# Two layers of a hybrid streaming-encoder trunk: the recurrence paced one channel tile a slot, splits of the indexer queries queued a unit later, key copies moved to VectorE

## The chip, the core and the metric

The kernel runs on one core of one Trainium2 chip. The metric is the device time of one execution in microseconds (us), measured around the whole program; below it is given as the median of three executions. The engines are TensorE (PE; its weight loads are listed apart as PEld), VectorE (DVE), ScalarE (ACT), GpSimd (POOL) and SyncE (SP), which here issues nearly all DMAs.

## What is computed

Two layers over a sequence of 512 tokens with 1024 channels, in fp32. Each layer normalises the input, projects it once into ten pieces and runs three branches: (A) a gMLP gate, (B) sparse attention, in which a small relu indexer picks 128 keys for each query, (C) a gated linear recurrence (RG-LRU). The branches are projected, gated, summed and projected back; a ConvFFN follows. Cut to the lines that matter for the change:

```python
gu, gv, q, k, v, qi, ki, wi, lx, lg = jnp.split(h @ w_in[l], IN_SPLITS, axis=-1)
# (B) the indexer: 8 heads of 64, one shared key
qi = apply_rope(qi.reshape(bsz, seq, IDX_HEADS, IDX_DIM), cos_i, sin_i)
ki = apply_rope(ki[:, :, None, :], cos_i, sin_i)[:, :, 0, :]
logits = jnp.einsum('bqhd,bsd->bqhs', qib, ki) * (IDX_DIM ** -0.5)
score = jnp.einsum('bqhs,bqh->bqs', jax.nn.relu(logits), wib) * (IDX_HEADS ** -0.5)
...
# (C) the recurrence, on xc = causal_dwconv(lx, conv_w, conv_b)
r = jax.nn.sigmoid(einsum(xg, w_r) + b_r)
i = jax.nn.sigmoid(einsum(xg, w_i) + b_i)
log_a = -LRU_C * r * softplus(-lam)
a = jnp.exp(log_a)
b = jnp.sqrt(-jnp.expm1(2.0 * log_a)) * (i * xc)
h_t = a_t * h_(t-1) + b_t          # associative_scan over the sequence
y_c = h * jax.nn.gelu(lg)
```

## The kernel before, in words

**Products and weights.** Activations lie with channels on the 128 partitions and the 512 tokens along the free axis, as four or eight channel tiles. An fp32 operand is split into two fp32r halves, high and low, and `mm3` (L127 to L132) makes each product of three fp32r matmuls: high by high (L130), high by low (L131), low by high (L132; which operand is the weight differs by the phase). `mm` (L124 to L126) is a plain fp32 matmul; the recurrence's gates use it. All weights come as a stream of units, one 512 KB tile each: `Stream` (L144) loads a tile through SP's DMA queue into one of six staging buffers `wst`, copies it on ACT to `wh` (the high half) and subtracts on DVE to get `wl` (the low half), five units ahead of its use, in six buffers. A unit is 24 matmuls of 512 columns. Within a layer the units come in this order: lx (4), qi (4), ki, v (4), lg (4), gv (4), gu (4), the gates and projections of branch C, k and q (8), the branches A and B, wo, up, dn. Results land in PSUM, a pool of eight banks that are handed out in turn; a matmul into a bank waits until what was read from it before has been read. Helpers record most elementwise work, so the profile names the helper's line: L104 is ACT's `act`, L109 its `copy`, L112 `tt` (`tensor_tensor`, on DVE unless POOL is passed as `G_`; a `split` is a copy and a `tt`), L116 `ts`, L121 `stt`.

**Order of the work.** After nearly every unit the program calls `B.pump(budget)` (L214). Each call is a slot: generators that were added as background tasks run in their order until the budget is spent. A task that yields a positive number has used that much of the budget; one that yields -n sleeps n slots. A low task, the modulation rows of a later norm (`mod_task`, L309), advances one accumulation (L121, 128x1024) a slot. The order of the instructions on each engine is the order in which this program writes them.

**The stretch that the change touches** (`layer`, L767). The lx units make the four tiles `xc` through a causal convolution. Then the recurrence `lru` (L595) is added as a background task and sleeps four slots. Each of the four qi units runs `rope` (L524): two 64-row copies on ACT from PSUM, a product on DVE, a product and a sum on POOL. The sum is then split: a copy on ACT, a subtraction on POOL. The ki unit (L795 to L810) does a rope for the single key, copies the indexer weights `wr`, splits the key, and makes from each half two masked keys: `k0` by a scale on ACT, `k1` by a memset on POOL and two 32-row copies on ACT. Four v units follow; their four banks collect all tokens over all four units. After each of the first three the slot has a budget of 5.0. The lg units make the gate of the recurrence.

**The recurrence** computes for each tile two gate matmuls (L601) into two banks with a sigmoid each (ACT, L603), then exponentials and tangents hyperbolic (L610, L611), a maximum and a root (L615, L616), two products and the scan (L619 to L622), and, when lg is there, the product with it and a split. With its sleep of four and budgets of 2.0 and 5.0, tiles 0 and 1 get their gates behind ki, tiles 2 and 3 behind v0. The `indexer` (L534) sleeps three slots from ki on, transposes `wr` (L540 copies it from PSUM), and then makes the scores of three query blocks i = 1, 2, 3 with 128 (i + 1) columns: for each head a product of three matmuls, a ReLU on ACT and an accumulation on DVE; a copy of the score row on ACT (L561) ends a block. The choice of the 128 largest follows on DVE.

Of the kernel before, what the change touches and what calls it, by code (L numbers as in the profile page):

```python
# [67 lines left out]
def trunk_kernel(ctx: ExitStack, tc: tile.TileContext, x, cc, wm, wu, cp, rows, gmw, gmb, lruw, cst, out):  # L68
# [17 lines left out]
    V, A_, G_, T_ = nc.vector, nc.scalar, nc.gpsimd, nc.tensor  # L86
# [6 lines left out]
    def S(dt=F32, shape=None):  # L93
        return sp.tile(shape or [P, 512], dt, tag="S", name=nm("s"), bufs=NS)
# [13 lines left out]
    def copy(o, i, scale=1.0):  # L108
        A_.activation(o, i, AF.Copy, scale=scale)  # L109

    def tt(o, a, b, op, eng=None):
        (eng or V).tensor_tensor(o, a, b, op)  # L112
# [7 lines left out]
    def stt(o, a, s, b, op0, op1):  # L120
        V.scalar_tensor_tensor(o, a, s, b, op0=op0, op1=op1)  # L121

    M, AD, SU = ALU.mult, ALU.add, ALU.subtract
# [130 lines left out]
    cos_i, sin_i = ks[:, K_CI:K_CI + 512], ks[:, K_SI:K_SI + 512]  # L254
# [141 lines left out]
    def col(kind, budget=2.0):  # L396
        if carry:
            p = carry.pop(0)
            return p
        p = bank()  # L400
        w = W.get(kind)
        cm(p, w)
        return p
# [120 lines left out]
    def rope(p, cs, sn):  # L524
        r = S()
        copy(r[0:64], p[64:128])
        copy(r[64:128], p[0:64])
        d = S()
        tt(d, p, cs, M)
        tt(r, r, sn, M, G_)  # L530
        tt(d, d, r, AD, G_)
        return d
# [61 lines left out]

    def lru(xc, lw, s84, wts, gl, res):  # L595
        rr, ii = [], []
        yield -4
        for t in range(4):
            for wi_, ob, lst in ((0, O_BR, rr), (1, O_BI, ii)):
                p = bank()  # L600
                mm(p, wts[wi_][:, t * P:(t + 1) * P], xc[t], True, True)  # L601
                o = S()
                act(o, p, AF.Sigmoid, bias=lw[:, ob + t:ob + t + 1])  # L603
                lst.append(o)
            yield 1.2
        aa = []
        for t in range(4):
            tt(ii[t], ii[t], xc[t], M, G_)
            a = S()
            act(a, rr[t], AF.Exp, scale=s84[:, t:t + 1])  # L610
            act(rr[t], rr[t], AF.Tanh, scale=s84[:, 4 + t:5 + t])  # L611
            aa.append(a)
            yield 1.2
        for t in range(4):
            V.tensor_scalar(rr[t], rr[t], 1e-34, None, op0=ALU.max)  # L615
            act(rr[t], rr[t], AF.Sqrt)  # L616
            yield 0.6
        for t in range(4):
            stt(rr[t], aa[t], 1.0, rr[t], AD, M)  # L619
            tt(ii[t], ii[t], rr[t], M)  # L620
            yield 1.2
            V.tensor_tensor_scan(xc[t], aa[t], ii[t], 0.0, M, AD)  # L622
            yield 0.6
        while len(gl) < 4:
            yield -1
        for t in range(4):
            tt(xc[t], xc[t], gl[t], M)
            yh, yl = S(F32R), S(F32R)
            split(yh, yl, xc[t], G_)
            res.append((yh, yl))  # L630
            gl[t] = None
            yield 0.6
# [134 lines left out]
    def layer(l):  # L767
# [7 lines left out]
        xc = []  # L775
        for t in range(4):
            p = col("lx")
            o = S()
            c = lambda tap: lw[:, O_CW + tap * 4 + t:O_CW + tap * 4 + t + 1]
# [6 lines left out]
        B.add(lru(xc, lw, s84, lrw, gl, yc))  # L786
        del xc, lrw
        qi = []
        for j in range(4):
            r = rope(col("qi"), cos_i, sin_i)  # L790
            a, c = S(F32R), S(F32R)
            split(a, c, r, G_)
            qi.append((a, c))
            B.pump(2.0)
        p = col("ki")  # L795
        kr = rope(p, cos_i, sin_i)
        wr = S()
        copy(wr[0:32], p[32:64])
        kp = S(F32R), S(F32R)
        split(*kp, kr)  # L800
        k0 = S(F32R), S(F32R)
        k1 = S(F32R), S(F32R)
        for i in range(2):
            f = kp[i].bitcast(F32)
            G_.memset(k1[i].bitcast(F32), 0.0)
            act(k0[i], f, AF.Identity, scale=ks[:, K_M:K_M + 1])
            copy(k1[i][32:64], f[0:32])
            copy(k1[i][96:128], f[64:96])
        kih = [k0, k1]
        B.pump(2.0)  # L810
        bias, ready = {0: bias0}, {0: 0}
        idx = indexer(qi, kih, wr, bias, ready)
        del qi, kih, kr, k0, k1, kp, wr, r, a, c
        B.add(idx)

        def tok_units(kind, budget=3.0):
            ps = [bank() for _ in range(TB)]
            for t in range(4):
                w = W.get(kind)
                for tb in range(TB):  # L820
                    for i in range(2):
                        k = 2 * t + i
                        mm3(ps[tb], hs(k, tb * P, P), w(i * 512, 512), k == 0, k == KT - 1)
                if t < 3:
                    B.pump(budget)
            return ps

        v = []
        for p in tok_units("v", 5.0):
            o = S()  # L830
            copy(o, p)
            v.append(o)

        for t in range(4):
            p = col("lg")
# [29 lines left out]
        for t in range(4):  # L865
            p = col("gu")
# [58 lines left out]
        v = kk = None  # L925
# [97 lines left out]
    for hf in range(2):  # L1023
        p = bank()
# [14 lines left out]
    for hf in range(2):  # L1039
        p = bank()  # L1040
# [30 lines left out]
    for k in range(KT):  # L1071
        if k in (0, 2):
            c = slice(k, 2 if k == 0 else KT)
            tt(bc[:, c], pc[k > 1][:, c], par0[:, O_SH + c.start:O_SH + c.stop], AD)
        p = hb[k].rearrange("p a b -> p (a b)")
# [132 lines left out]
```

## Time and profile before

| | before |
|---|---|
| median of 3 executions | 1763.41 us (1762.78 to 1765.32) |
| the profiled execution | 1764.15 us, of which the profile's span is 1762.3 |
| PE busy | 1706.9 us, 97% |
| DVE busy | 1131.7 us, 64% |
| ACT busy | 703.0 us, 40% |
| POOL busy | 275.5 us, 16% |
| granted TensorE clock, mean | 0.987 of full |
| read from and written to HBM | 219.02 and 4.19 MB, 127 GB/s |

The span runs from the first to the last instruction that the profiler shows; the profiled execution's own time lies 1.85 us above it, and 0.74 us above the median. The shares are means over the whole program, in which stretches with different limits follow each other. A matmul of 512 columns is listed with 0.39 us from its start to its modelled end, while the next one starts 0.23 us behind it: matmuls overlap, so PE's pace is read from starts.

### The profile page before, as it was taken

Reading aid. Unit: us, or ns where it says so; the run is one execution under the profiler, and the core shown is the slowest. Engines: PE = TensorE matmul, PEld = TensorE weight load, DVE = VectorE, ACT = ScalarE, POOL = GpSimd, SP = SyncE. Lnnn points to the kernel's source line nnn. Section 1 sums busy time; section 2 is a strip of 40 time slices with the busy share of each in tenths; the row PEclk is TensorE's granted clock in tenths of the full one; section 3 lists DMA queues with packets and bytes.
Section 4 is the critical chain, followed back from the end, with each engine's and each line's share of the span. In section 5 each row is a group of like instructions: output and inputs, shape, how many; then the busy total and the mean of one; then the engine's idle time right before and its main releaser. Section 6 shows DMA issues by size and latency. Waiting matters only on the chain.

```text
span 1762.3 us, 20815 instructions
## 1 busy us (share of the span) xinstructions
PE 1706.9 (97%) x7972; PEld 1414.3 (80%) x7972; DVE 1131.7 (64%) x1667; ACT 703.0 (40%) x1075; POOL 275.5 (16%) x208
## 2 busy tenths in 40 slices
PE   4979999999999999999998999999999999999998
PEld 2858888888889888888887788887888888888886
DVE  6848789854456898553466577986745676445443
ACT  3574423443344343332344743253433443333331
POOL 3141011310000211110004111041200011221000
PEclk8989999999999999999999999999999999999999
DMA  8646322332413776233234452324424255232311
GB/s 339 194 143 197 114 93 96 120 120 72 145 60 107 229 226 193 96 98 100 74 134 144 138 185 72 97 94 156 144 84 143 73 167 156 96 97 95 108 48 48
DMA packets 67643, 224.57 MB, mean 127 GB/s; under 512 B 7636, under 2 KB 8020, under 8 KB 67416
## 3 DMA queue, kind: packets, MB, share of 16 engines
q1 hardware_dynamic: 67248, 223.10, 39.2%
q8 instruction: 62, 1.02, 0.2%
q14 instruction: 37, 0.30, 0.1%
q10 hardware_dynamic: 296, 0.14, 0.0%
HBM read 219.02 MB, written 4.19 MB: 127 GB/s over the span
## 4 chain that ended last, share of the span: by engine, by line
PE 87%; DVE 5%; ACT 3%; issue 2%; POOL 2%; DMA 1%; ACTq 0%; DVEq 0%; POOLq 0%
PE ps L130 27%; PE ps L132 27%; PE ps L131 27%; PE ps L126 4%; POOL s L112 2%; DVE acc L121 1%; DVE s L121 1%; ACT wh L109 1%; ACT s L109 1%; DVE wl L112 1%; ACT junk L106 1%; DVE s L112 1%; PE ps L717 0%; PE ps L372 0%; DMA wst<-in_wu_dram 0%
## 5 line engine op out<-in xcount | busy, mean ns | idle before, releaser
L130 PE MATMUL ps<-hh,wh 128*128 128x512 f32 (+1 forms) x1608 | 605.7, 377 | 0.8 <-ACT s L109 0.8
L131 PE MATMUL ps<-hl,wh 128*128 128x512 f32 (+1 forms) x1608 | 600.7, 374 | 2.5 <-DVE hl L112 2.5
L132 PE MATMUL ps<-hh,wl 128*128 128x512 f32 (+1 forms) x1608 | 600.7, 374 | 0.0
L112 DVE TENSOR_TENSOR wl<-wst,wh 128x1024 fp32r<-128x1024 f32 x277 | 357.8, 1294 | 254.6 <-ACT wh L109 254.3
L109 ACT ACTIVATE wh<-wst 128x1024 fp32r<-128x1024 f32 x278 | 291.2, 1052 | 172.4 <-PE ps L132 104.6
L131 PEld LDWEIGHTS ps<-hl,wh 128*128 128x128 f32 x1608 | 303.2, 189 | 57.2 <-DVE hl L112 3.4
L130 PEld LDWEIGHTS ps<-hh,wh 128*128 128x128 f32 x1608 | 303.2, 189 | 55.6 <-ACT s L109 1.2
L132 PEld LDWEIGHTS ps<-hh,wl 128*128 128x128 f32 x1608 | 303.0, 188 | 53.9
L112 POOL TENSOR_TENSOR s<-s,s 128x512 f32<-128x512 f32 (+1 forms) x118 | 203.7, 1733 | 676.0 <-DVE s L121 479.1
L121 DVE SCALAR_TENSOR_TENSOR s<-ps,lw,s 128x511 f32<-128x511 f32 (+3 forms) x208 | 155.1, 748 | 140.6 <-ACT s L104 135.1
L104 ACT ACTIVATE s<-ps,lw 128x512 f32<-128x512 f32 x112 | 84.4, 766 | 261.4 <-PE ps L132 258.4
L130 PE MATMUL ps<-wh,s 128*128 128x512 f32 x416 | 162.4, 390 | 0.0
L132 PE MATMUL ps<-wh,s 128*128 128x512 f32 x416 | 161.9, 389 | 0.0
L131 PE MATMUL ps<-wl,s 128*128 128x512 f32 x416 | 161.9, 389 | 0.0
L243 POOL TENSOR_TENSOR sm<-sm,mhalf 128x1 f32<-128x1 f32 x40 | 22.8, 573 | 524.9 <-DVE sm L118 491.1
L121 DVE SCALAR_TENSOR_TENSOR acc<-ms,cact,acc 128x1024 f32<-128x1024 f32 x70 | 93.9, 1342 | 9.6 <-DMA ms<-in_wm_dram 9.4
L109 ACT ACTIVATE s<-s 128x512 fp32r<-128x512 f32 (+2 forms) x100 | 61.1, 618 | 94.9 <-DVE s L112 45.1
L104 ACT ACTIVATE s<-ps,bg 128x512 f32<-128x512 f32 x48 | 33.0, 687 | 149.1 <-PE ps L132 149.1
L132 PEld LDWEIGHTS ps<-wh,s 128*128 128x128 f32 x416 | 78.1, 188 | 16.2
L131 PEld LDWEIGHTS ps<-wl,s 128*128 128x128 f32 x416 | 78.1, 188 | 16.1
L130 PEld LDWEIGHTS ps<-wh,s 128*128 128x128 f32 x416 | 78.1, 188 | 15.9
L109 ACT ACTIVATE s<-ps 64x512 f32<-64x512 f32 (+6 forms) x104 | 55.0, 543 | 61.8 <-PE ps L132 44.1
(128 smaller groups left out, 1808.2 us busy)
## 6 DMA issues: line engine op xcount, KB each, us to landing
wst<-in_wu_dram SPq DMA_DIRECT2D x286, 512.0 KB, 3.7
ms<-in_wm_dram SPq DMA_DIRECT2D x80, 512.0 KB, 4.0
s<-in_rows_dram SPq DMA_DIRECT2D x34, 256.0 KB, 5.7
m<-in_wm_dram SPq DMA_DIRECT2D x16, 512.0 KB, 7.6
s<-in_x_dram SPq DMA_DIRECT2D x16, 256.0 KB, 5.1
xd<-s SPq DMA_DIRECT2D x8, 256.0 KB, 2.1
s<-xd SPq DMA_DIRECT2D x8, 256.0 KB, 5.9
out_dram<-s SPq DMA_DIRECT2D x8, 256.0 KB, 2.0
```

Of the source, the lines that this page charges most:

```text
L104: A_.activation(o, i, f, bias=bias, scale=scale)
L106: A_.activation(o, i, f, bias=bias, scale=scale, accum_out=acc)
L109: A_.activation(o, i, AF.Copy, scale=scale)
L112: (eng or V).tensor_tensor(o, a, b, op)
L121: V.scalar_tensor_tensor(o, a, s, b, op0=op0, op1=op1)
L126: T_.matmul(o, l, r, start=start, stop=stop)
L130: T_.matmul(o, lh, rh, start=start, stop=False)
L131: T_.matmul(o, lh, rl, start=False, stop=False)
L132: T_.matmul(o, ll, rh, start=False, stop=stop)
L243: G_.tensor_tensor(y, h, mhalf, ALU.pow)
```

## The change

The program orders the same arithmetic differently; nothing is computed that was not computed before.

- `lru` sleeps two slots instead of four, so its first gates come behind qi2. It then makes the gates of one tile a slot (tile 1 behind qi3, tile 2 behind ki, tile 3 behind v0), tells its pace by sleeps and no longer by costs, runs the exponentials of tiles 0 and 1 in the slot of tile 3 and those of tiles 2 and 3 with all roots one slot later, and the scans in two slots of two. The product of the input gate with `xc` moves from POOL to DVE.
- The split of each qi tile is written one unit later, behind the next unit's rope; that of the last behind ki's rope.
- The four 32-row copies into `k1` move from ACT to DVE.
- The v slots have a budget of 3.0 instead of 5.0.

```diff
--- before.py
+++ after.py
@@ -594,7 +594,7 @@
 
     def lru(xc, lw, s84, wts, gl, res):
         rr, ii = [], []
-        yield -4
+        yield -2
         for t in range(4):
             for wi_, ob, lst in ((0, O_BR, rr), (1, O_BI, ii)):
                 p = bank()
@@ -602,25 +602,27 @@
                 o = S()
                 act(o, p, AF.Sigmoid, bias=lw[:, ob + t:ob + t + 1])
                 lst.append(o)
-            yield 1.2
+            if t < 3:
+                yield -1
         aa = []
         for t in range(4):
-            tt(ii[t], ii[t], xc[t], M, G_)
+            tt(ii[t], ii[t], xc[t], M)
             a = S()
             act(a, rr[t], AF.Exp, scale=s84[:, t:t + 1])
             act(rr[t], rr[t], AF.Tanh, scale=s84[:, 4 + t:5 + t])
             aa.append(a)
-            yield 1.2
+            if t == 1:
+                yield -1
         for t in range(4):
             V.tensor_scalar(rr[t], rr[t], 1e-34, None, op0=ALU.max)
             act(rr[t], rr[t], AF.Sqrt)
-            yield 0.6
         for t in range(4):
+            if t % 2 == 0:
+                yield -1
             stt(rr[t], aa[t], 1.0, rr[t], AD, M)
             tt(ii[t], ii[t], rr[t], M)
-            yield 1.2
             V.tensor_tensor_scan(xc[t], aa[t], ii[t], 0.0, M, AD)
-            yield 0.6
+        yield -1
         while len(gl) < 4:
             yield -1
         for t in range(4):
@@ -786,16 +788,24 @@
         B.add(lru(xc, lw, s84, lrw, gl, yc))
         del xc, lrw
         qi = []
-        for j in range(4):
-            r = rope(col("qi"), cos_i, sin_i)
+
+        def split_qi(r):
             a, c = S(F32R), S(F32R)
             split(a, c, r, G_)
             qi.append((a, c))
+
+        r = None
+        for j in range(4):
+            rj = rope(col("qi"), cos_i, sin_i)
+            if j:
+                split_qi(r)
+            r = rj
             B.pump(2.0)
         p = col("ki")
         kr = rope(p, cos_i, sin_i)
         wr = S()
         copy(wr[0:32], p[32:64])
+        split_qi(r)
         kp = S(F32R), S(F32R)
         split(*kp, kr)
         k0 = S(F32R), S(F32R)
@@ -804,13 +814,13 @@
             f = kp[i].bitcast(F32)
             G_.memset(k1[i].bitcast(F32), 0.0)
             act(k0[i], f, AF.Identity, scale=ks[:, K_M:K_M + 1])
-            copy(k1[i][32:64], f[0:32])
-            copy(k1[i][96:128], f[64:96])
+            V.tensor_copy(k1[i][32:64], f[0:32])
+            V.tensor_copy(k1[i][96:128], f[64:96])
         kih = [k0, k1]
         B.pump(2.0)
         bias, ready = {0: bias0}, {0: 0}
         idx = indexer(qi, kih, wr, bias, ready)
-        del qi, kih, kr, k0, k1, kp, wr, r, a, c
+        del qi, kih, kr, k0, k1, kp, wr, r, rj, p
         B.add(idx)
 
         def tok_units(kind, budget=3.0):
@@ -826,7 +836,7 @@
             return ps
 
         v = []
-        for p in tok_units("v", 5.0):
+        for p in tok_units("v", 3.0):
             o = S()
             copy(o, p)
             v.append(o)
```

Three places in the order of the instructions show it. In the names below, `ps` is a PSUM bank, `s` a tile of 128x512, `wst`, `wh` and `wl` the stages of a weight; the last number of a name tells the buffers apart.

First ACT in layer 0, the units qi1 and qi2 as they stand before (rope copies from PSUM, the split of the same unit, a weight):

```order
L109 ACTIVATE s_132_616<-ps_128_585 64x512 x2
L109 ACTIVATE s_134_623<-s_133_619 128x512
L109 ACTIVATE wh_138_631<-wst_110_467 128x1024
L109 ACTIVATE s_141_661<-ps_137_630 64x512 x2
L109 ACTIVATE s_143_668<-s_142_664 128x512
L109 ACTIVATE wh_147_676<-wst_116_506 128x1024
```

and with the change:

```order
L109 ACTIVATE s_139_657<-ps_135_626 64x512 x2
L109 ACTIVATE s_141_664<-s_131_615 128x512
L104 ACT_TABLE_LOAD
L104 ACTIVATE s_145_673<-ps_144_671,lw_21_132 128x512
L104 ACTIVATE s_147_677<-ps_146_675,lw_21_132 128x512
L109 ACTIVATE wh_149_680<-wst_116_506 128x1024
L109 ACTIVATE s_152_710<-ps_148_679 64x512 x2
L109 ACTIVATE s_154_717<-s_140_660 128x512
L104 ACTIVATE s_157_724<-ps_156_722,lw_21_132 128x512
L104 ACTIVATE s_159_728<-ps_158_726,lw_21_132 128x512
L109 ACTIVATE wh_161_731<-wst_122_545 128x1024
```

The split now reads a tile of the unit before (`s_131` belongs to qi1, in the unit of qi2), and the gates of tile 0 and tile 1, with the table load, stand behind qi2 and qi3.

Second, ACT at the ki unit of layer 0, before:

```order
L109 ACTIVATE s_158_749<-ps_154_718 64x512 x2
L109 ACTIVATE s_160_756<-ps_154_718 32x512
L109 ACTIVATE s_161_758<-s_159_752 128x512
L104 ACTIVATE s_163_762<-s_161_758,ks_77 128x512
L109 ACTIVATE s_165_764<-s_161_758 32x512 x2
L104 ACTIVATE s_164_763<-s_162_759,ks_77 128x512
L109 ACTIVATE s_166_765<-s_162_759 32x512 x2
L109 ACTIVATE s_167_774<-acc_98_417 128x512
L109 ACTIVATE s_169_778<-acc_98_417 128x512
L104 ACT_TABLE_LOAD
L104 ACTIVATE s_179_798<-ps_178_796,lw_21_132 128x512
L104 ACTIVATE s_181_802<-ps_180_800,lw_21_132 128x512
```

and with the change, up to the first weight behind it:

```order
L109 ACTIVATE s_164_761<-ps_160_730 64x512 x2
L109 ACTIVATE s_166_768<-ps_160_730 32x512
L109 ACTIVATE s_167_770<-s_153_713 128x512
L109 ACTIVATE s_169_774<-s_165_764 128x512
L104 ACTIVATE s_171_778<-s_169_774,ks_77 128x512
L104 ACTIVATE s_172_779<-s_170_775,ks_77 128x512
L109 ACTIVATE s_175_790<-acc_98_417 128x512
L109 ACTIVATE s_177_794<-acc_98_417 128x512
L104 ACTIVATE s_187_814<-ps_186_812,lw_21_132 128x512
L104 ACTIVATE s_189_818<-ps_188_816,lw_21_132 128x512
L109 ACTIVATE wh_194_824<-wst_129_586 128x1024
```

The four 32-row copies and the table load are gone from here, and two sigmoids, of tile 2, stand where four stood.

Third, DVE in the lg units of layer 0. Before, the scans are long done, modulation accumulations and weight splits alternate, and the indexer's weights are copied (`wi`) behind the products with lg:

```order
L112 TENSOR_TENSOR wl_244_1126<-wst_216_971,wh_243_1125 128x1024
L121 SCALAR_TENSOR_TENSOR acc_171_782<-ms_241_1121,cact_83,acc_171_782 128x1024
L112 TENSOR_TENSOR s_97_412<-s_97_412,s_225_1036 128x512
L112 TENSOR_TENSOR s_105_454<-s_105_454,s_234_1083 128x512
L112 TENSOR_TENSOR s_111_493<-s_111_493,s_240_1119 128x512
L112 TENSOR_TENSOR s_117_532<-s_117_532,s_246_1155 128x512
L540 COPY wi_255_1178<-ps_256_1179 128x32
L844 MEMSET s_257_1185 64x4x64
L112 TENSOR_TENSOR wl_264_1195<-wst_224_1010,wh_263_1194 128x1024
```

With the change the chains of tiles 2 and 3 end here, behind the modulation rows, and the indexer's weights and first accumulations follow:

```order
L112 TENSOR_TENSOR s_182_804<-ps_228_1036,s_182_804 128x512
L121 SCALAR_TENSOR_TENSOR mod_227_1035<-s_182_804,s_183_806 128x512
L112 TENSOR_TENSOR s_184_808<-ps_229_1041,s_184_808 128x512
L121 SCALAR_TENSOR_TENSOR mod_227_1035<-s_184_808,s_185_810 128x512
L121 SCALAR_TENSOR_TENSOR s_187_814<-s_208_907,s_187_814 128x512
L112 TENSOR_TENSOR s_189_818<-s_189_818,s_187_814 128x512
L624 SCALAR_TENSOR_TENSOR s_111_493<-s_208_907,s_189_818 128x512
L121 SCALAR_TENSOR_TENSOR s_199_859<-s_209_911,s_199_859 128x512
L112 TENSOR_TENSOR s_201_863<-s_201_863,s_199_859 128x512
L624 SCALAR_TENSOR_TENSOR s_117_532<-s_209_911,s_201_863 128x512
L540 COPY wi_230_1052<-ps_231_1053 128x32
L112 TENSOR_TENSOR wl_234_1061<-wst_206_877,wh_233_1060 128x1024
L121 SCALAR_TENSOR_TENSOR acc_179_798<-ms_226_1032,cact_83,acc_179_798 128x1024
L116 TENSOR_SCALAR s_238_1095<-s_238_1095,wi_230_1052 128x256
```

Between the modulation rows and the copy of `wi` now stand the two products and scans (L624) of tiles 2 and 3, and the first score row (L116) comes one weight split and one accumulation behind that copy.

## Rows read from the trace of the kernel before

**Rows 1.** The page, busy time, share of the span and number of instructions by engine.
```profile
PE 1706.9 (97%) x7972; PEld 1414.3 (80%) x7972; DVE 1131.7 (64%) x1667; ACT 703.0 (40%) x1075; POOL 275.5 (16%) x208
```

**Rows 2.** Waits of PE: ended by what; us in total, times, longest us.
```profile
PE ps L126 <- ACT s L104: 12.2, 2, 7.3
...
PE ps L130 <- ACT s L109: 7.0, 3, 4.6
...
PE ps L130 <- ACT s L104: 1.5, 2, 1.1
PE ps L130 <- DVE wi L540: 0.2, 1, 0.2
```

**Rows 3.** Windows, layer 0: us, busy (instructions) by engine, granted clock, DMA share, GB/s.
```profile
97.35:100.38 3.03, 3.03 (x10) 1.35 (x8) 2.82 (x3) 1.36 (x3) 2.08 (x3) 1.00 0.26 95
100.38:106.60 6.22, 4.66 (x21) 3.36 (x19) 2.75 (x3) 3.35 (x5) 4.52 (x4) 1.00 0.52 167
106.60:115.55 8.95, 1.65 (x6) 1.04 (x6) 2.74 (x4) 7.75 (x12) 1.97 (x3) 0.72 0.59 171
115.55:121.29 5.74, 5.74 (x8) 2.40 (x9) 2.71 (x2) 4.15 (x7) 3.64 (x3) 0.54 0.38 109
```

**Rows 4.** Windows of the same places in layer 1.
```profile
956.38:965.60 9.22, 4.66 (x20) 3.36 (x18) 5.53 (x5) 4.73 (x8) 6.52 (x6) 0.91 0.51 152
965.60:973.39 7.79, 2.93 (x7) 1.84 (x7) 1.89 (x2) 6.61 (x10) 1.96 (x3) 0.50 0.40 129
973.39:978.58 5.19, 5.19 (x8) 2.25 (x9) 2.53 (x2) 4.14 (x7) 3.10 (x3) 0.60 0.02 4
```

**Rows 5.** Timeline of PE behind the first gates: start, us, engine, line, operation, shape.
```profile
100.38 0.79 PE L130 MATMUL ps<-wh,hh 128*128 128x512 f32 x1
101.01 0.40 PE L131 MATMUL ps<-wl,hh 128*128 128x512 f32 x1
101.24 0.39 PE L132 MATMUL ps<-wh,hl 128*128 128x512 f32 x1
```

**Rows 6.** Timeline of ACT, qi units; in brackets the idle time before and its releaser.
```profile
90.18 1.05 ACT L109 ACTIVATE wh<-wst 128x1024 fp32r<-128x1024 f32 x1
91.25 1.20 ACT L109 ACTIVATE s<-ps 64x512 f32<-64x512 f32 x2
...
95.94 0.63 ACT L109 ACTIVATE s<-s 128x512 fp32r<-128x512 f32 x1 [3.49 <-POOL s L112]
```

**Rows 7.** Timeline of ACT, ki's unit and the first sigmoids.
```profile
103.85 1.20 ACT L109 ACTIVATE s<-ps 64x512 f32<-64x512 f32 x2
...
111.07 1.26 ACT L109 ACTIVATE s<-s 32x512 fp32r<-32x512 f32 x2
...
113.52 1.28 ACT L104 ACT_TABLE_LOAD   x1
114.81 2.42 ACT L104 ACTIVATE s<-ps,lw 128x512 f32<-128x512 f32 x4
```

**Rows 8.** Timeline of POOL in a qi unit.
```profile
90.35 1.30 POOL L112 TENSOR_TENSOR s<-s,s 128x512 fp32r<-128x512 f32 x1 [0.74 <-ACT s L109]
92.53 1.15 POOL L112 TENSOR_TENSOR s<-s,ks 128x512 f32<-128x512 f32 x1 [0.88 <-ACT s L109]
93.76 2.15 POOL L112 TENSOR_TENSOR s<-s,s 128x512 f32<-128x512 f32 x1
```

**Rows 9.** Timeline of DVE, the end of tile 0's chain and a weight split.
```profile
133.57 0.69 DVE L112 TENSOR_TENSOR s<-s,s 128x512 f32<-128x512 f32 x1
134.30 1.22 DVE L622 TENSOR_TENSOR_SCAN s<-s,s 128x512 f32<-128x512 f32 x1
135.44 1.20 DVE L112 TENSOR_TENSOR wl<-wst,wh 128x1024 fp32r<-128x1024 f32 x1
```

**Rows 10.** Timeline of ACT, the copy of the first score row.
```profile
178.94 0.42 ACT L109 ACTIVATE s<-s 128x256 f32<-128x256 f32 x1 [2.52 <-DVE s L121]
```

**Rows 11.** Windows, the top-k stretch (240 to 340 us), sum and mean of five.
```profile
sum 100.00, PE 100.00 PEld 82.62 DVE 91.30 ACT 37.70 POOL 21.86; mean PE 20.00 PEld 16.52 DVE 18.26 ACT 7.54 POOL 4.37
```

## The prediction

> **What bounds the kernel now.** I read the page's busy times first: TensorE (PE) is busy for 1706.9 of 1762.3 us [rows 1], so only what PE waits for, or does slowly, can move the end. The waits of PE came next [rows 2]. Its largest entries are the fp32 gate matmuls of the recurrence (L126, ended by ScalarE's L104, the sigmoids) and the f32r matmuls ended by ScalarE's L109 copies. Both mean a PSUM bank that ScalarE (ACT) had not read yet.
>
> Cut into windows, both lie in one place of each layer, right behind the ki unit. In layer 0 the first gate group takes 3.03 us; v0's first 18 matmuls then run 4.66 of 6.22 us, the last 6 run 1.65 of 8.95 us, and the second gate group, the same four matmuls as the first, takes 5.74 us [rows 3]. The granted clock falls to 0.72 and 0.54 of full there, after the waits, so part of the time runs at the lower level (1.2 of 2.4 GHz). Layer 1 repeats it: 4.66 of 9.22, 2.93 of 7.79, and 5.19 us for the second group [rows 4].
>
> Why the banks are late is read from ACT's own timeline. In each qi unit ACT copies the rope halves, then stands 3.5 us for GpSimd (POOL), then splits that same unit and converts one weight tile [rows 6]. The rope pairs start at 91.25 and, two units later, at 103.85 [rows 6, 7]: 6.3 us a unit, where PE needs 24 matmuls x 0.23 = 5.5 us [rows 5]. So ACT falls back 0.8 us a unit, and ki's rope starts 6.5 us after PE ended ki at 97.35. From there to the first sigmoid it is another 114.81 - 103.85 = 10.96 us, all in front of sigmoids whose matmuls were done at 100.38 [rows 3, 7].
>
> **The change, part by part.** *Splits one unit later.* ACT's copy now needs a POOL result that is a unit old. ACT's work in a qi unit is rope 1.20 + split 0.63 + weight 1.05 = 2.9 us [rows 6, 7], 4.1 us with two sigmoids (a group of four took 2.42, 0.6 each); POOL's is 1.30 + 1.15 + 2.15 = 4.6 us [rows 8]. Both are under 5.5, so I take ACT as on time when ki ends: the wait of v0 for ki's bank (1.56 and 4.56 us) goes. The bound against it: if all three POOL instructions were stretched as the third is (2.15 beside DVE, about 1 us over its neighbours), POOL would need 6.5 us a unit and lag 1 us a unit, 4 us at ki; the splits' unit of slack (5.5 us) covers that.
>
> *Sigmoids, one channel tile a unit.* The gate pairs of tiles 0 and 1 now stand ahead of qi3 and ki, that of tile 2 behind ki, that of tile 3 behind v0. v0's banks are then freed by sigmoids a unit old. ACT's path from ki's rope to tile 2's first sigmoid loses 4 copies (2 x 1.26) and one table load (1.28): 10.96 - 3.80 = 7.2 us, 7.8 with the sigmoid itself [rows 7]. As built, lg0 is the next user of that bank, at 1.5 + 0.4 + 5.5 (v0) + 1.5 + 0.4 + 16.5 (v1 to v3) = 25.8 us after ki: 18 us of cover. Tile 3's banks come from ki's short copy and tile 1's sigmoid, both earlier still. So the waits of 7.30 and 7.79 - 2.93 = 4.86 us go, and the second gate group returns from 5.74 and 5.19 to 3.03. In layer 1, six matmuls that took 2.93 at clock 0.50 return to at most the 1.65 of layer 0.
>
> ACT's table load moves into qi2's unit: 4.1 + 1.28 = 5.4 us against a unit of 5.5 + 1.5 for the gate pair, so it is hidden there, and copies between the sigmoids cost no second load: a weight copy already stands between two sigmoids of the old queue. The Trainium skill (ScalarE: Activation LUTs, What ACT_TABLE_LOAD costs) puts a switch of sets at about 2.66 us, a drain of 1.38 included, and asks to finish one set before the next (Rules for kernel authors), which speaks against spreading the sigmoids; the trace shows 1.28 and a sigmoid 0.01 us behind it [rows 7]. By the page's price qi2's unit would hold 6.8 us of ACT work against 7.0, still not in PE's way.
>
> *Work moved between engines.* Per layer DVE gets four products (0.69 each [rows 9], 2.8 us) from POOL and four 32-row copies from ACT. Their price on DVE is not in the trace: as little as nothing beside the wait for POOL's memset, at most the 0.69 of a full-height product; I take 0.6, what ACT needs for the same copy (1.26 / 2), so 2.4 us. None of it is on PE's path: DVE stood idle for ACT in this stretch, and the copies' readers are the indexer's odd heads, 38 us later.
>
> *Added on PE.* The gate matmuls now come in four groups instead of two. The first f32r matmul behind a group starts the second 0.63 us later instead of 0.23 [rows 5]: 2 more switches a layer, 4 x 0.40 = 1.6 us.
>
> *Recurrence and indexer in the lg units.* The scans of tiles 2 and 3 move behind lg0, and the indexer starts two units earlier, behind lg1, eight heads a slot. What is late next is DVE. Counted from ki's end: the old run's first scan ends 134.30 + 1.22 - 114.81 = 20.7 us after the first sigmoid, so here at latest 20.7 after tile 3's sigmoid, which follows the gate pair behind v0 (1.5 + 0.4 + 5.5 + 1.5 = 9): at 29.7. Then come the second tile's chain (2.6), two weight splits and an accumulation (3 x 1.2), four modulation rows (4 x 0.69), tiles 2 and 3 (5.2) and the copy of the indexer weights: 44 us. Another weight split and accumulation (2.4) and eight 256-wide accumulations (eight times 0.69 at most, half of that at least) end at 49.2 to 52. ACT's copy of that score row (0.42, [rows 10]) waits for it, and the ReLUs of the next eight heads stand behind the copy; the first frees the bank that lg3 needs. PE is at lg3 at 25.8 + 5.5 (lg0) + 1.5 + 5.5 (lg1) + 2.8 + 5.5 (lg2) + 4.1 = 50.7 (eight heads are 24 matmuls of 256 columns, then of 384, at half and three quarters of 0.23). So PE waits 0 to 2 us here in layer 0; I take 0, since half the columns lies nearest half the time. In layer 1 the modulation rows come later and leave about 2 us of slack.
>
> The old bursts cost 1.5 and 0.2 us [rows 2]; I leave them in, since bursts remain.
>
> **The sum.** Layer 0: 1.56 + 7.30 + (5.74 - 3.03) = 11.57. Layer 1: 4.56 + 4.86 + (2.93 - 1.65) + (5.19 - 3.03) = 12.86. Together 24.4, less 1.6 for the switches: 22.8 us. The profiled execution took 1764.15 us (1762.3 of span and 1.85 around it), which gives 1741.3; the median of the runs, 1763.41, is 0.74 lower, so I predict 1740.6. The upper bound of the gain is 24.4 + 1.7 = 26.1 (bursts gone, switches free): 1737.3.
>
> **The rivals.** *DVE late in the lg units.* The copy of the score row becomes a wait that PE feels. For it: DVE's backlog above has 0 to 2 us to spare, and ACT already waits 2.52 us for DVE at that copy [rows 10]. Against it: PE did not stop there. If DVE is another 6 us late in both layers, PE waits about 5.4 + 4: 1750.
>
> *Only one of the two waits goes*, because ACT is late at ki for another reason than the splits, so that tile 3 or v0 still waits: about half the sum, 1752. Against it: ACT waits for nothing but PE and POOL in rows 6 and 7.
>
> *The gain is given back in the top-k stretch, and more.* DVE is busy for 91.3 of 100 us there [rows 11], and PE now arrives 11.4 us a layer earlier. Weights are converted five units ahead (27.5 us), and DVE's split is half of that. Were DVE to fall back on some 30 units by more than (27.5 + 11.4) / 30 = 1.3 us each, PE would wait for weights and the kernel would be slower; at 1.5 us it is 45 - 27.5 = 17.5 a layer, 1776. Between, it would come out level. Against it: the same work fitted before with 100 - 91.3 = 8.7 us in 100 to spare, PE has no wait there in rows 2, and the indexer begins two units sooner.
>
> **How the numbers follow.** Forecast 0.75 (1736.5 to 1746), DVE late 0.14, half 0.05, top-k level 0.03 or slower 0.03. The range 1736.5 to 1749 holds the forecast and most of the first rival. A difference under 0.2% (3.5 us) is about what a measurement of this kernel can't tell from none. Faster by more: 0.75 + 0.14 + 0.05 = 0.94; level 0.03; slower 0.03.
>
> **What would show it.** Right: PE's waits for L104 and L109 behind ki are gone or under 1 us in both layers, the clock stays at 1.0 there, the four gate groups take 1.5 us each, and ACT's rope pairs follow PE's units at 5.5 us (7 with a gate pair). Wrong: a PE wait ended by L104 at the start of lg3 or of an indexer head (DVE late), one ended by L109 in v0 (ACT still late), or waits for wl in the top-k stretch.

## The result, and the profile after

The changed kernel takes 1739.12 us, the median of four executions (1738.39 to 1739.35), against 1763.90 us for the kernel before in the same comparison (1762.78 to 1765.32). The ratio is 0.9858, with a 95% interval from 0.9841 to 0.9875: 24.8 us less. The profiled execution took 1739.10 us with a span of 1737.3, which is 25.0 us less span than before.

The page's busy times, where [rows 1] stand before:

```profile
PE 1699.6 (98%) x7972; PEld 1411.5 (81%) x7972; DVE 1150.2 (66%) x1683; ACT 695.3 (40%) x1067; POOL 274.7 (16%) x200
```

PE issues the same number of matmuls and is busy for 7.3 us less, since fewer of them run at the lower clock (granted clock 1.00 below, where it fell to 0.72, 0.54 and 0.50 in [rows 3, 4]). DVE has 16 instructions more, ACT and POOL 8 fewer each: the eight key copies and the eight products of both layers. The waits of PE (what ended them; us in total, times, longest), against [rows 2]:

```profile
PE ps L126 <- DMA s<-in_rows_dram: 12.5, 1, 12.5
...
PE ps L130 <- ACT s L109: 0.8, 1, 0.8
PE ps L130 <- ACT s L104: 0.4, 1, 0.4
```

The 12.2 us for the sigmoids are gone, and so are 6.2 of the 7.0 us for L109 (the 0.8 left is an attention unit in layer 1 that waited before too). The 12.5 us are the start of the program, before the first unit. Windows of four gate pairs (tiles 0, 2 and 3 of layer 0, tile 3 of layer 1) and, in the fourth row, of the stretch from v1 to the start of the lg units (us; busy by PE, PEld, DVE, ACT, POOL; granted clock; DMA share; GB/s), where [rows 3, 4] had two groups of four a layer:

```profile
87.54:88.85 1.31, 1.31 (x5) 0.59 (x4) 1.31 (x2) 1.10 (x2) 1.31 (x1) 1.00 0.62 216
101.95:103.27 1.32, 1.32 (x6) 0.60 (x4) 0.00 (x0) 1.11 (x2) 0.30 (x1) 1.00 0.70 124
109.16:110.47 1.31, 1.31 (x5) 0.59 (x4) 1.27 (x4) 1.28 (x3) 0.00 (x0) 1.00 0.00 0
110.47:127.24 16.77, 16.77 (x74) 13.68 (x73) 11.86 (x16) 16.58 (x24) 0.00 (x0) 1.00 0.49 157
952.54:953.86 1.32, 1.32 (x6) 0.59 (x4) 1.26 (x4) 1.10 (x2) 0.55 (x2) 1.00 0.00 0
```

The clock stays at 1.00, a pair takes 1.31 us, and PE has no gap. The fourth row also shows what has become full in its place: ACT is busy for 16.58 of 16.77 us.

Counted by PE's starts, the time from the first lx unit to v1 fell from 73.78 to 61.74 us in layer 0 (12.04) and from 64.38 to 51.22 in layer 1 (13.16); the rest of the token mixing, up to the first matmul of the gMLP, gave 0.71 and 0.79 more. The start took 1.2 us longer in this execution and the end 0.5; what lies between the two layers' stretches is equal to 0.03 us. Together 12.75 + 13.95 + 0.03 - 1.22 - 0.51 = 25.0.

ACT in layer 0: qi2's unit, ki's rope, tile 2's sigmoids and the copy of the first score row (start, us, engine, line, operation; in brackets the idle time before and its releaser), against [rows 6, 7, 10]:

```profile
87.74 1.19 ACT L109 ACTIVATE s<-ps 64x512 f32<-64x512 f32 x2 [0.50 <-PE ps L132]
88.95 0.63 ACT L109 ACTIVATE s<-s 128x512 fp32r<-128x512 f32 x1
89.61 1.28 ACT L104 ACT_TABLE_LOAD   x1
90.90 1.27 ACT L104 ACTIVATE s<-ps,lw 128x512 f32<-128x512 f32 x2
...
102.15 1.19 ACT L109 ACTIVATE s<-ps 64x512 f32<-64x512 f32 x2 [3.25 <-PE ps L132]
...
109.52 1.26 ACT L104 ACTIVATE s<-ps,lw 128x512 f32<-128x512 f32 x2
...
150.90 0.42 ACT L109 ACTIVATE s<-s 128x256 f32<-128x256 f32 x1 [2.14 <-DVE s L121]
```

ACT now waits for PE: ki's rope starts 0.2 us behind ki's end at 101.95, where it was 6.5 us late. The split of the tile before follows the rope with no wait (88.95). From the rope to tile 2's first sigmoid it is 7.37 us. The copy of the score row waits 2.14 us for DVE, whose rows in front of it are these:

```profile
143.99 0.16 DVE L540 COPY wi<-ps 128x32 f32<-128x32 f32 x1
144.07 1.21 DVE L112 TENSOR_TENSOR wl<-wst,wh 128x1024 fp32r<-128x1024 f32 x1
145.20 1.28 DVE L121 SCALAR_TENSOR_TENSOR acc<-ms,cact,acc 128x1024 f32<-128x1024 f32 x1
146.39 0.34 DVE L116 TENSOR_SCALAR s<-s,wi 128x256 f32<-128x256 f32 x1
146.85 4.01 DVE L121 SCALAR_TENSOR_TENSOR s<-s,wi,s 128x256 f32<-128x256 f32 x7
```

The row is done at 150.86. PE comes to lg3 at 152.15, without a wait in layer 0 and with one of 0.37 us in layer 1.

### The profile page after: what moved, and what is told of

It reads as the page before. It is cut to its first block, busy times and chain, and to the rows that moved or that the text cites. A ratio compares the mean times of both kernels' runs of the same rounds, so it can differ in the third digit from the quotient of the medians.

```text
span 1737.3 us, 20819 instructions
## 1 busy us (share of the span) xinstructions
PE 1699.6 (98%) x7972; PEld 1411.5 (81%) x7972; DVE 1150.2 (66%) x1683; ACT 695.3 (40%) x1067; POOL 274.7 (16%) x200
## 4 chain that ended last, share of the span: by engine, by line
PE 91%; DVE 4%; ACT 2%; issue 2%; DMA 1%; POOL 0%; ACTq 0%; DVEq 0%; POOLq 0%
PE ps L130 29%; PE ps L132 29%; PE ps L131 29%; PE ps L126 4%; DVE acc L121 1%; DVE s L112 1%; DVE s L121 1%; ACT s L104 1%; ACT junk L106 1%; ACT wh L109 1%; PE ps L719 0%; PE ps L372 0%; DVE wl L112 0%; DMA craw<-in_c_dram 0%; DMA ks<-in_cst_dram 0%
## 5 line engine op out<-in xcount | busy, mean ns | idle before, releaser
L112 DVE TENSOR_TENSOR wl<-wst,wh 128x1024 fp32r<-128x1024 f32 x277 | 363.9, 1317 | 217.5 <-ACT wh L109 217.4
L109 ACT ACTIVATE wh<-wst 128x1024 fp32r<-128x1024 f32 x278 | 291.2, 1053 | 179.9 <-PE ps L132 104.6
L243 POOL TENSOR_TENSOR sm<-sm,mhalf 128x1 f32<-128x1 f32 x40 | 22.8, 573 | 533.8 <-DVE sm L118 486.2
L109 ACT ACTIVATE s<-s 128x512 fp32r<-128x512 f32 (+1 forms) x92 | 55.7, 616 | 77.7 <-DVE s L112 45.4
L109 ACT ACTIVATE s<-ps 64x512 f32<-64x512 f32 (+6 forms) x104 | 54.4, 542 | 63.7 <-PE ps L132 52.0
```

Source lines behind the costliest of these rows:

```text
L243: G_.tensor_tensor(y, h, mhalf, ALU.pow)
```

## The experiments

The change has three parts: the splits a unit later, the new pacing of the recurrence (with its product on DVE and the v budget), and the key copies on DVE. With the new pacing the v budget, 3.0 or 5.0, changes the place of no instruction, since the recurrence then spends none of it; the run with the pacing alone keeps 5.0. Each run below was compared with the kernel before on the same chip (medians 1763.9 to 1765.1). The gains in us:

| splits late | new pacing | keys on DVE | median | gain |
|---|---|---|---|---|
| yes | yes | yes | 1739.12 | 24.8 |
| | yes | yes | 1752.69 | 12.5 |
| yes | | yes | 1750.23 | 14.9 |
| yes | yes | | 1745.74 | 19.4 |
| yes | | | 1756.80 | 8.0 |
| | yes | | 1760.96 | 3.8 |
| | | yes | 1759.90 | 4.9 |

The second to fourth rows leave one part out, the last three have one part alone. Alone the parts give 8.0 + 3.8 + 4.9 = 16.7 us, together 24.8. Taken out of the whole, each costs more than it gives alone: 12.3 (splits), 9.9 (pacing), 5.4 (keys), as differences of the gains.

**Without the pacing.** `lru` as before in all its lines, and the budget of the v units; splits and key copies as in the change:

```diff
-        yield -2
+        yield -4
...
-        for p in tok_units("v", 3.0):
+        for p in tok_units("v", 5.0):
```

> The changed kernel with the recurrence paced as before (sleep of four slots, two tiles a slot, budget of 5.0 in the v slots); splits a unit late and key copies on DVE stay. Theory A, one lag: both old waits come from ACT being 6.5 and 9.5 us late at ki, so once the splits are late and the key copies gone, the old pacing finds ACT in time but for little: ki's rope 0.2 us behind ki, first sigmoid 7.4 to 8.0 us later plus the table load of 1.28, done some 9.5 to 10.0 us behind ki, where PE wants the bank at 8.9: waits of about 0.6 and 1.2 us, and the indexer's bursts as before (0.7 and 0.8 us): about 1743 us. Theory B, parts that add up as in the prediction's sum (the pacing removes 7.30 and 4.86 us): about 1753 us.

Measured: 1750.23 us, ratio 0.9918 [0.9901, 0.9934], between the two theories. PE's waits at the second gate group of each layer, in PE's timeline:

```profile
110.70 0.70 PE L126 MATMUL ps<-s,s 128*128 128x512 f32 x1 [2.60 <-ACT s L104]
...
959.76 2.07 PE L126 MATMUL ps<-s,s 128*128 128x512 f32 x2 [4.65 <-ACT s L104]
```

ACT and POOL in layer 0 of the same run:

```profile
99.25 1.20 ACT L109 ACTIVATE s<-ps 64x512 f32<-64x512 f32 x2 [2.63 <-PE ps L132]
...
105.08 0.63 ACT L109 ACTIVATE s<-s 128x512 fp32r<-128x512 f32 x1 [2.77 <-POOL s L112]
...
109.96 2.42 ACT L104 ACTIVATE s<-ps,lw 128x512 f32<-128x512 f32 x4
```

```profile
90.62 2.07 POOL L112 TENSOR_TENSOR s<-s,ks 128x512 f32<-128x512 f32 x1
...
97.12 2.07 POOL L112 TENSOR_TENSOR s<-s,ks 128x512 f32<-128x512 f32 x1
...
102.60 1.08 POOL L112 TENSOR_TENSOR s<-s,ks 128x512 f32<-128x512 f32 x1
```

ACT is on time at ki (99.25, with PE's unit ended at 99.05), so the late splits do what they should. But POOL's same product starts 6.5 us apart (90.62, 97.12): without a gate pair in between a unit is 5.4 us, POOL falls behind, and the key's split waits 2.77 us for it. The sigmoids come 10.7 us after the rope. Theory A missed this wait. The pacing is worth more than its sigmoids: by spreading the pairs it gives POOL 7.2 us for a unit.

**With the splits in their own unit.** The new pacing and the key copies stay:

```diff
-            rj = rope(col("qi"), cos_i, sin_i)
-            if j:
-                split_qi(r)
-            r = rj
+            r = rope(col("qi"), cos_i, sin_i)
+            a, c = S(F32R), S(F32R)
+            split(a, c, r, G_)
+            qi.append((a, c))
```

> The changed kernel with each qi tile's split in its own unit again; new pacing and key copies on DVE stay. Theory A, one lag: ACT is late again (about 3.9 us at ki in layer 0, 9.9 in layer 1, where POOL is late from the first qi unit on), but in layer 0 every bank is free in time, so no wait there; in layer 1 waits of about 2.3 us in v0 and 1.2 at the gates of tile 3: about 1743 us. Theory B, parts that add up (the splits remove 1.56 and 4.56 us): a wait in both layers, about 1745 us.

Measured: 1752.69 us, ratio 0.9933 [0.9918, 0.9948], slower than both theories had it. PE's waits:

```profile
110.68 1.12 PE L126 MATMUL ps<-s,s 128*128 128x512 f32 x2 [0.99 <-ACT s L109]
157.25 0.50 PE L130 MATMUL ps<-hh,wh 128*128 128x512 f32 x1 [2.52 <-ACT s L104]
...
958.71 0.50 PE L130 MATMUL ps<-wh,hh 128*128 128x512 f32 x1 [2.15 <-ACT s L104]
962.80 1.13 PE L126 MATMUL ps<-s,s 128*128 128x512 f32 x2 [1.56 <-ACT s L109]
...
1007.55 0.50 PE L130 MATMUL ps<-hh,wh 128*128 128x512 f32 x1 [3.27 <-ACT s L104]
```

The waits in v0 and at tile 3's gates in layer 1 (2.15 + 1.56 = 3.7) are as theory A had them. In layer 0 it had none: it took ACT to be 3.9 us late at ki, and ACT is 6.6 us late there (its rope at 108.09, PE's unit ended at 101.46). What neither theory had are the two waits at lg3, where the ReLUs stand behind the copy of the score row, and two of 0.41 and 0.71 us at heads of the indexer in layer 0, whose banks DVE has not read yet. They suggest that ACT's lateness is not forgotten after the gates, but goes on through the exponentials and roots to DVE's scans, and from there to the first score row. The next runs test it.

**With the key copies on ACT:**

```diff
-            V.tensor_copy(k1[i][32:64], f[0:32])
-            V.tensor_copy(k1[i][96:128], f[64:96])
+            copy(k1[i][32:64], f[0:32])
+            copy(k1[i][96:128], f[64:96])
```

> The changed kernel with the four 32-row key copies back on ACT. As the prediction has it (2.5 us on ACT with 18 us of cover, none of it on PE's path): about 1739 us. Theory A with DVE full: the trace of the changed kernel shows DVE without a pause from 127.57 to 150.86 us, and before that it waits only for ACT, which has no pause from 106 to 129; 2.5 us more on ACT move DVE's scans and so the first score row 2 to 2.5 us later, and PE waits at lg3 or just ahead of it, about 1.9 us in layer 0 and 2.7 in layer 1: about 1743 us.

Measured: 1745.74 us, ratio 0.9891 [0.9876, 0.9906]. PE's waits at lg3 in both layers, then the score row's copy in layer 0:

```profile
154.14 0.50 PE L130 MATMUL ps<-hh,wh 128*128 128x512 f32 x1 [2.04 <-ACT s L104]
...
999.64 0.80 PE L130 MATMUL ps<-hh,wh 128*128 128x512 f32 x1 [2.76 <-ACT s L104]
```

```profile
153.30 0.42 ACT L109 ACTIVATE s<-s 128x256 f32<-128x256 f32 x1 [4.74 <-DVE s L121]
```

The waits have the size (1.9 and 2.7 us) and the place that the second expectation gave; the median is 2.7 us above its 1743. So the 2.5 us that these copies take on ACT do lie on PE's path, 45 us later, and what the prediction called cover is not there. From these runs came theory C: ACT behind ki, the recurrence on DVE and the first score row are one chain, and PE pays for every us by which it is late.

**One part alone**, three runs of the kernel before with one part of the diff each. First the splits:

> The kernel before with one part of the change: the splits a unit late (old pacing, key copies on ACT). Theory C, one chain: every us by which ACT is late behind ki is paid by PE further on, at the second gate group here; so this is the run without the new pacing (waits of 2.60 and 4.65 us there) plus the 2.5 us of key copies on ACT in each layer: about 5.1 and 7.2 us of wait at the second gate group, none for ki's bank in v0, about 1755 us. The prediction's sum (the splits remove only 1.56 and 4.56 us): about 1759 us with 7.3 and 4.9 us left.

Measured 1756.80 us, ratio 0.9954 [0.9939, 0.9969]. The waits for the sigmoids are 5.21 and 7.11 us, together in this row of the waits of PE; no wait for ki's bank is left:

```profile
PE ps L126 <- ACT s L104: 12.3, 2, 7.1
```

> The kernel before with the new pacing of the recurrence alone (splits in their own unit, key copies on ACT). Theory C: the run with only the splits put back, plus 2.5 us of ACT a layer; the bank that tile 3's gates want is freed ahead of the key copies, so the waits in v0 and at tile 3 stay (about 1 us in layer 0, 3.7 in layer 1), and the 2.5 us come at lg3, through DVE and the score row: 2.5 + 2.5 and 3.3 + 2.5 us there, about 1758 us. The prediction's sum (the pacing removes 7.30 and 4.86 us and the slow second groups): about 1748 us.

Measured 1760.96 us, ratio 0.9977 [0.9967, 0.9986]. The waits of PE:

```profile
PE ps L130 <- ACT s L104: 12.0, 3, 5.7
...
PE ps L130 <- DVE s L112: 2.4, 1, 2.4
```

Of the 12.0 us, 2.14 lie in v0 of layer 1 and 4.21 and 5.69 at lg3. The pacing alone moves most of the sigmoids' wait (12.2 us before) from the gates to lg3, behind DVE's score row. Theory C was near (1758 us), the prediction's sum (1748) far off. The run is 3 us longer than theory C had it, and two things in its trace add to the time that theory C left out: the 2.36 us of layer 0, in which a head of the indexer waits for the bank of a modulation row that DVE has not read, and the lower clock behind the longer waits. Around lg3 of layer 0 the granted clock is 0.83 here; in the run with the splits in their own unit it is 1.00:

```profile
155.00:165.00 10.00, 5.79 (x20) 4.56 (x20) 8.84 (x16) 4.40 (x10) 0.14 (x1) 0.83 0.58 191
```

> The kernel before with the key copies on DVE alone. Theory C: ACT's path to the first sigmoid loses 4 copies of 0.63, so the wait at the second gate group falls from 7.3 to 4.8 and from 4.9 to 2.4 us: about 1760 us. If the path is set by POOL or DVE at that place (the memset, the subtraction), so that the copies were hidden: about 1765 us.

Measured 1759.90 us, ratio 0.9969 [0.9957, 0.9981]. The sigmoid waits are 4.61 and 2.29 us:

```profile
PE ps L130 <- ACT s L109: 7.0, 3, 4.6
PE ps L126 <- ACT s L104: 6.9, 2, 4.6
```

The 2.5 us of the copies come off the path in full, and the 7.0 us ahead of them do not move. Apart from the 2.36 us, all three runs put their waits where theory C had them.

**DVE as the carrier.** In the run with the key copies on ACT, the modulation accumulations rest at every second slot:

```diff
+        B.every = 2
         v = []
...
             B.pump(4.0)
...
+        B.every = 1
```

> The run with the key copies on ACT, and the modulation accumulations at every second slot only, from the first v unit to the last lg unit (the rest of them follows later). Theory C says that ACT's lateness reaches PE through DVE, which has no pause ahead of the first score row: in layer 0 one accumulation of 1.2 us less stands there, so the wait at lg3 falls from 2.04 to about 0.8 us, in layer 1 from 2.76 to about 1.6 (one less) or 0.4 (two less). If ACT itself is what PE waits for, both waits stay: about 1745 us as before.

Measured 1742.90 us, ratio 0.9871 [0.9855, 0.9888]; PE's wait at lg3 in layer 0:

```profile
152.21 0.50 PE L130 MATMUL ps<-hh,wh 128*128 128x512 f32 x1 [0.83 <-ACT s L104]
```

ACT's work is the same as in the run with the key copies on ACT. DVE has two accumulations fewer, but one of them stood where DVE waits for ACT's weight copy anyway (3.42 us now, 2.23 then). The other stood ahead of the score row, in the stretch without a pause, and the wait falls by its 1.2 us, from 2.04 to 0.83. ACT was only the messenger: what PE waits for is DVE's row. In layer 1 the wait at lg3 went too, but one of 2.35 us for the copy of `wi` (L540) appeared ahead of it. The same rest in the changed kernel:

> The changed kernel with the same rest for the modulation accumulations. The 0.37 us of wait in layer 1 goes, nothing else is gained: about 1738.7 us. If the accumulations that follow later crowd DVE in the choice of the 128 largest, waits of PE for weights or for ACT there: slower by up to 4 x 1.2 us a layer.

Measured 1739.54 us, ratio 0.9853 [0.9839, 0.9868]: not to be told from the change. No wait is left in the stretch, but 1.3 and 0.2 us appear at 1264 us, at the modulation row that now comes later. So none of these versions beats the changed kernel by more than can be told.

**The product back on POOL:**

```diff
-            tt(ii[t], ii[t], xc[t], M)
+            tt(ii[t], ii[t], xc[t], M, G_)
```

> The changed kernel with the product of the input gate and the tile back on POOL. On DVE the four products lie where it waits for ACT's weight copies (2.65 and 2.23 us of idle time just behind them), so taking them away wins nothing there; POOL has time for them. As the prediction has it: about 1739 us, no new wait. If POOL, slow beside DVE (2.1 us where a product alone takes 1.1), brings the products late to the scans, the first score row is late by as much and PE waits at lg3: 1740 to 1743 us.

Measured 1742.86 us, ratio 0.9871 [0.9857, 0.9886], with 1.11 and 2.49 us of wait at lg3. The way was none of the two expected. DVE in this run, then POOL:

```profile
106.67 0.63 DVE L817 CAST s<-s 32x512 fp32r<-32x512 f32 x1
107.31 1.42 DVE L818 CAST s<-s 32x512 fp32r<-32x512 f32 x1
108.75 1.40 DVE L817 CAST s<-s 32x512 fp32r<-32x512 f32 x1
110.16 1.43 DVE L818 CAST s<-s 32x512 fp32r<-32x512 f32 x1
```

```profile
106.99 4.31 POOL L112 TENSOR_TENSOR s<-s,s 128x512 f32<-128x512 f32 x3
```

With the change, the same casts on DVE:

```profile
108.36 0.42 DVE L818 CAST s<-s 32x512 fp32r<-32x512 f32 x1
...
109.23 0.42 DVE L818 CAST s<-s 32x512 fp32r<-32x512 f32 x1
```

POOL's products fall on the key casts, and each of the last three casts takes 1.4 us in place of 0.42, as long as one of the three products (4.31 / 3 = 1.44). The Trainium skill, SBUF — State Buffer (Who interferes with whom), states that a copy or cast can use both port pairs of DVE, that POOL shares the second pair, and that whoever issues first holds it for its whole instruction while the other is blocked. These rows agree: one cast for each product.

The 3 us do not reach PE by themselves. The next weight loads wait for DVE to be done with the buffers (SP's queue stands 12.5 us for it there, 8.3 with the change), so a modulation weight lands late, just ahead of the maxima:

```profile
120.75 1.28 DVE L121 SCALAR_TENSOR_TENSOR acc<-ms,cact,acc 128x1024 f32<-128x1024 f32 x1 [2.49 <-DMA ms<-in_wm_dram]
```

With the change there is no wait at that place; in layer 1 of this run it is 2.80 us. Without the 2.49 us the maxima would have started at 119.46, before ACT had loaded the table for the roots (120.98). With them DVE reaches the maxima ahead of the roots late (ACT waits 1.42 and 1.79 us for them), and so the scans and the score row.

**The indexer's slot.** One slot earlier, then one later:

```diff
-        yield -3
+        yield -2
```

> The changed kernel with the indexer one slot earlier (a sleep of two slots instead of three). This is the rival 'DVE late in the lg units', made larger. If DVE sets when a score row is done: the first row ends at about 148.4 us (the scans of tiles 2 and 3 stand ahead of it, two instructions of 1.2 us less), while PE wants lg2's bank at about 145.7: waits of 3 to 4 us a layer ended by ACT, about 1746 us. If DVE has room, the bursts only move: about 1739 us.

Measured 1743.10 us, ratio 0.9876 [0.9861, 0.9890]. In layer 1 PE waits 3.39 us, as expected; ACT's copy of the score row there:

```profile
992.58 0.42 ACT L109 ACTIVATE s<-s 128x256 f32<-128x256 f32 x1 [6.09 <-DVE s L121]
```

In layer 0 it waits not at all. There the modulation rows take part of the slot's budget, so only six of the eight heads ran in it and the row ended a slot later.

> The changed kernel with the indexer one slot later (a sleep of four slots). DVE then has one more unit of PE (5.4 us) and one more pair of its own (2.4 us) ahead of the first score row: 3 us of slack, so the 0.37 us of wait that is left in layer 1 goes; the rest of the kernel as it is: about 1738.7 us, not to be told from 1739. If the later start delays the choice of the 128 largest and PE comes to wait for it: slower, by up to 5 us a layer.

Measured 1743.39 us, ratio 0.9878 [0.9861, 0.9894]. This expectation failed: the wait at lg3 went, but five others came (4.3 us), since now the second score row meets a DVE that has the products with lg, a memset and the splits of a modulation row in front of it and between its heads (in layer 1 the modulation rows in place of the splits); layer 0:

```profile
171.91 0.52 ACT L109 ACTIVATE s<-s 128x384 f32<-128x384 f32 x1 [6.59 <-DVE s L121]
```

So the rival of the prediction, DVE late in the lg units, is real on either side of the slot that the indexer has: a slot earlier at the first score row, a slot later at the second.

## Why the prediction was right, and where its steps failed

The forecast was 1740.6 us, the median 1739.12; the sum was 22.8 us, and the profiled execution gave 25.05. Point by point:

- **What bounds the kernel, and ACT's lag.** Right. ACT follows PE at 0.2 us, both waits are gone in both layers, and the clock stays at 1.00. The lag was only half worked out: 0.8 us a unit makes about 2.6 of the 6.5 us at ki, over three units. Another 3.7 arose at once in the first qi unit, where before the change the split waited longest for POOL, which itself waited for DVE:

```profile
83.34 0.63 ACT L109 ACTIVATE s<-s 128x512 fp32r<-128x512 f32 x1 [6.35 <-POOL s L112]
```

- **The table load.** In qi2's unit ACT is busy for 5.4 us, as worked out, and the load costs 1.28 us with the sigmoid 0.01 behind it. The Trainium skill (ScalarE: Activation LUTs, What ACT_TABLE_LOAD costs) gives about 2.66 for a switch; the drain of 1.38 that it counts in shows on neither side of this row, and the measured 1.28 decides.
- **ACT's path from ki.** 7.2 us predicted, 7.37 measured.
- **POOL under 5.5 us a unit.** Wrong: the bound (6.5) was right and the value taken (4.6) was not. The run without the pacing shows 6.5 us. It did no harm in the change only because gate pairs stretch the units to 7.2 us.
- **The price of the casts on DVE.** 2.4 us predicted; 0.63 + 3 x 0.42 = 1.9 measured.
- **The gate groups.** The mis-sized term. 1.6 us were charged for two more switches a layer, and these switches cost nothing. Each fp32 gate matmul is two records, and PE's weight loads show one record every 0.43 us; here from the third record of the pair at 87.54 on:

```profile
87.97 0.19 PEld L126 LDWEIGHTS ps<-s,s 128*128 128x128 f32 x1 [0.24 <-issue]
88.40 0.19 PEld L126 LDWEIGHTS ps<-s,s 128*128 128x128 f32 x1 [0.24 <-issue]
88.83 0.19 PEld L130 LDWEIGHTS ps<-hh,wh 128*128 128x128 f32 x1 [0.24 <-issue]
89.25 0.19 PEld L131 LDWEIGHTS ps<-hl,wh 128*128 128x128 f32 x1 [0.24 <-issue]
```

  By these rows the 0.40 us that the prediction read as the price of a switch belong to the last fp32 record, which is still at work behind the start of the first f32r matmul. So a group costs 0.43 us a record however it is cut: two groups of four took 2 x (3.03 + 0.40) = 6.86 us a layer [rows 3, 5], the four pairs 4 x (1.31 + 0.40) = 6.84.
- **The DVE chain of the lg units.** Measured from ki's end: the first scan ends at 28.3 us (at latest 29.7 predicted), the score row at 48.9 (49.2 to 52), PE is at lg3 at 50.2 (50.7). The choice of no wait in layer 0 was right. In layer 1, where 2 us of slack were expected, PE waits 0.37: the modulation rows are gone from there, but DVE splits a modulation row (1.28 us) and waits 1.33 us for a modulation weight, so the score row again ends at 48.9 us, and PE, without the rows, would be at lg3 at 49.4.
- **The bursts of the indexer.** Left in, but all but gone: the stretch from v1 to the gMLP gave 0.71 + 0.79 us, the 0.37 left in layer 1 already taken off.
- **The matmuls behind the waits.** The sum left v0's 24 matmuls at 4.66 + 1.65 = 6.31 us; with the change they take 5.89 in both layers (103.27 to 109.16 in layer 0), 0.4 us a layer that the sum did not have. Before, the last of them ran at 0.72 and 0.50 of full clock [rows 3, 4].
- **The top-k stretch.** DVE is busy for 82.05 us between 240 and 340, in place of 91.30 [rows 11], and for 86.08 if the window moves with the work (228.5 to 328.5); PE has no wait there. That rival fell.

With 22.8 + 1.6 (switches) + 1.5 (bursts) + 0.8 (slow matmuls) the two stretches should give 26.7, and they gave 12.75 + 13.95 = 26.7. That the forecast lies within 1.5 us of the median is in part luck: the sum was 3.9 us short in the stretches, and a start and an end that were longer in this execution took 1.7 back.

Beside the term for the switches, a step failed that is not in the sum. The prediction wrote of the work moved between engines that "None of it is on PE's path", and that behind tile 2's sigmoid there were "18 us of cover". The cover was for the bank; for DVE, which takes the sigmoids' results, there is none. The reason that it gave, "DVE stood idle for ACT in this stretch", says the opposite: an engine that waits for ACT hands on ACT's lateness. Put back, the key copies cost 5.4 us and the product 2.5, as differences of the gains. The sum did not suffer since both were moved and the whole chain fitted, by the 0 to 2 us that the prediction had worked out for lg3; that is luck too, as no term of the sum asked for it. And it spoke of the removed waits as if each belonged to one part (1.56 and 4.56 us to the splits, 7.30 and 4.86 to the sigmoids' pace). The pacing alone gave 3.8 us, since the wait goes on to lg3. These waits belong to no single part: they are gone only when the whole chain fits.

## What to carry to other kernels

When an engine is late at one place, follow its results to the next user before calling anything behind it covered: here 2.5 us of ACT's lateness went through DVE nearly without a loss (2.04 us of wait in layer 0, 2.76 where 0.37 was there already in layer 1) and were paid 45 us later, and a third of the gain (24.8 against 16.7 us) showed only when all parts were in. Where parts of a change share a chain, cost the chain's end, not the parts. A slot that has almost no slack on either side, as the indexer's has, should be tried in both directions before it is called free.

## What was not expected of the hardware

A 32x512 cast on DVE took 0.42 us alone and 1.40 to 1.43 beside POOL's products, and POOL's 128x512 product 1.08 to 1.10 us alone and 2.07 to 2.08 beside DVE. Read from starts, one group of four fp32 gates takes 3.03 us where two pairs take 2 x 1.31 = 2.62, and a change from fp32 to f32r seems to cost 0.40. Both are one thing: records 0.43 us apart, the last of which lies behind the start of the next matmul.
